# A transformer kernel on one core: three norm boundaries get a fixed order on three engines

## The chip, the core and the metric

The kernel runs on one core of a Trainium2 chip. Its engines are TensorE (PE, with its weight loads PEld), VectorE (DVE), ScalarE (ACT), GpSimd (POOL) and SyncE (SP, which issues the weight transfers). The metric is the device time of one launch in microseconds; the kernel before took 2123.85 us (median of three runs, 2120.73 to 2124.13).

## The reference

512 tokens of width 1024 pass through two models one behind the other, in float32. The first is one block of sparse attention and retention with an MLP. The second has two layers: an mLSTM mixer with a convolutional FFN, then a shared key and value projection, then a forgetting attention ("fox") with a second convolutional FFN. In the second model each sublayer is

```
y = mixer(rmsnorm(x, g_pre));  x = x + rmsnorm(y, g_post)
h = rmsnorm(x, g_ffn);         x = x + rmsnorm(conv_ffn(h), g_ffn_post)
```

with `rmsnorm(x, g) = x * rsqrt(mean(x*x) + 1e-6) * g`. So behind each mixer and each FFN a product's result is normed over its 1024 columns, added to x, and x is normed again for the next product.

## The kernel before

Activations lie with features on the 128 partitions: x is eight tiles of 128 x 512 (`xt[0..7]`), one column per token. Each float32 operand is split into a rounded part and a remainder (`hi`, `lo` for activations by `split`, `wh`, `wl` for weights by `split_steps`, L153 to L174), and a product is three matmuls, hi·wh, lo·wh and hi·wl (`mm3`, L474 to L476).

Weights come in blocks of up to 2048 columns a partition, in the order in which the products use them (`WT.plan`). SP loads a block into one of two `raw` buffers. A block is split in parts of 1024: ACT writes `wh`, DVE subtracts to get `wl`, or POOL does where `on_pool` lists the part: three parts at each of the three boundaries below. There are four buffers for `wh` and four for `wl`. `WT.get` loads and splits one block ahead.

`post_norm` ends a mixer or an FFN: a product with eight output tiles, whose last block (two tiles of 8 k steps behind a mixer, one tile of 22 k steps behind an FFN) is done in two halves of 256 tokens (`gemm_halves`). For each output tile ACT squares it (`sq`), DVE copies it from PSUM (`Y`), and POOL adds the squares up. When the first half of the last tile is done, `finish(0)` sums the squares over features (PE transposes, a DVE reduction), takes root (ACT) and reciprocal (DVE), and PE spreads the factor over a PSUM tile. Then, for each of eight rows k and each half: DVE scales Y (L1432), DVE adds it to x (L1434), ACT writes `hi` of the next product (L1438), DVE writes `lo` (L1439).

The next product is `gemm` with `lead=2`: its first two blocks, four output tiles, are multiplied in halves before the factor of its own norm is known. Each of the 16 k steps (8 a half) needs one row's `hi` and `lo`. Meanwhile `stats` squares x, sums it and computes 1 / sqrt with a shift and three Newton steps on DVE (`rsqrt`); the four results are copied aside and scaled later.

There are three such boundaries: behind the mLSTM mixer (into FFN 0), behind FFN 0 (into the key and value projection), and behind the fox mixer (into FFN 1). The last FFN ends in `last_norm`, which is another code.

The order of the instructions on an engine is chosen by the framework's scheduler with its own costs, by readiness and by the order in the program, except where `in_order` chains the instructions of given engines in program order; the second model's FFN regions chain POOL alone.

Of the kernel before, what the change touches and what calls it, by code (L numbers as in the profile page):

```python
# [14 lines left out]
OP = mybir.AluOpType  # L15
# [99 lines left out]
class Weights:  # L115
# [40 lines left out]
    def split_steps(self, i):  # L156
# [7 lines left out]
        for k0 in range(0, kt, kk):  # L164
# [8 lines left out]
                res.append(tuple(t[:, k * cols:(k + 1) * cols].bitcast(F32R) for t in (h, l)))  # L173
            yield  # L174

    def _split(self, i):
        if i not in self.parts and i < len(self.plan):
            for _ in self.split_steps(i):
                pass

    def get(self, ahead=True):
        i = self.pos
        self.pos += 1
        self._dma(i)
        self._split(i)
        self._dma(i + 1)
        if not ahead:
            return self.parts[i]
        self._split(i + 1)
        self._dma(i + 2)  # L190
        return self.parts[i]
# [3 lines left out]
def block_kernel(ctx: ExitStack, tc: tile.TileContext, I, out):  # L195
    nc = tc.nc
    V, A, G, T = nc.vector, nc.scalar, nc.gpsimd, nc.tensor

    cst = ctx.enter_context(tc.tile_pool(name="cst", bufs=1))
    up = ctx.enter_context(tc.tile_pool(name="up", bufs=1))  # L200
    sm = ctx.enter_context(tc.tile_pool(name="sm", bufs=12))
    wr = ctx.enter_context(tc.tile_pool(name="wr", bufs=2))
    wh = ctx.enter_context(tc.tile_pool(name="wh", bufs=4))
    pg = ctx.enter_context(tc.tile_pool(name="pg", bufs=4, space=bass.MemoryType.PSUM))
    pss = ctx.enter_context(tc.tile_pool(name="pss", bufs=2, space=bass.MemoryType.PSUM))
    pst = ctx.enter_context(tc.tile_pool(name="pst", bufs=1, space=bass.MemoryType.PSUM))
# [3 lines left out]
    def unit(name="u", tag=None, dt=F32):  # L210
        tag = tag or TAGS.get(name, "u")
        return up.tile([128, 512], dt, tag=tag, name=name, bufs=BUFS[tag])

    def R(t):
        return t.bitcast(F32R)
# [65 lines left out]

    def plan_ffn(l):
        W = I["ffn_w_up_2"][l]
        WT.on_pool((1, 0), (1, 1), (3, 0))
        for b in range(22):
            WT.add(8, 256, [(lambda v: v[:, :, 0:128], ksrc(W, 0, 8, b * 128, 128)),
                            (lambda v: v[:, :, 128:256], ksrc(W, 0, 8, 2816 + b * 128, 128))])
        WT.add_fm(I["ffn_w_down_2"][l], 22, 4, 0, tail=True)

    plan_ffn(0)  # L290
    WT.on_pool((0, 1), (1, 0), (1, 1))
    WT.add_fm(kvw, 8, 2, 0)
    WT.add_tok(kvw, 1792, 272)
    WT.add_fm(kvw, 8, 2, 512)
# [67 lines left out]
    def gcol(nm, k, layer=0):  # L362
        b = vbase[nm] + layer * 8 + k
        return gv[:, b:b + 1]
# [38 lines left out]
    def tick(ns):  # L403
        if side[0] is not None:
            side[0].tick(ns)
# [9 lines left out]
    def token_sums(tiles, h=None):  # L415


        n = len(tiles)
        u = small(4 if h is None else 2, "ts")
        for b in (0, 1) if h is None else (h,):  # L420
            p = s_bank()
            for i in range(2):
                for m, t in enumerate(tiles):
                    c = 256 * b + 128 * i
                    T.transpose(p[:, (i * n + m) * 128:(i * n + m + 1) * 128], t[:, c:c + 128], ident)
            o = u[:, 2 * b:2 * b + 2] if h is None else u
            V.tensor_reduce(o, p[:, 0:256 * n].rearrange("p (i c) -> p i c", i=2), axis=AX.X, op=OP.add)
        return u
# [26 lines left out]
    def rstd_col(acc):  # L455
        u = token_sums(acc)
        V.tensor_scalar(u, u, 1.0 / 1024.0, 1e-6, op0=OP.mult, op1=OP.add)
        return rsqrt(u)
# [38 lines left out]
    def gemm(acts, nb, evac, lead=0, mid=None, halves=False, rest=None):  # L497

        KT = len(acts)
        b = 0
        if lead:
            w = [WT.get() for _ in range(lead)]
            m = mid() if mid else None
            if m:
                next(m)
            ps = [g_bank() for _ in range(2 * lead)]  # L510
            for ts in thalf if halves else (slice(0, 512),):
                for k in range(KT):
                    for c in range(2 * lead):
                        mm3(ps[c][:, ts], cut(w[c // 2][k], c % 2), [t[:, ts] for t in acts[k]], k == 0, k == KT - 1)
                        if c % 2:
                            tick(1280)
            if m:
                rest = settle(ps, m, evac)
            else:
                for c in range(2 * lead):  # L520
                    evac(c, ps[c])
            b = lead
        while b < nb:
            if KT <= 8:
                w = WT.get()
                for c in range(2):
                    ps = g_bank()
                    with in_order(tc, (mybir.EngineType.PE,)) if rest else nullcontext():
                        for k in range(KT):
                            mm3(ps, cut(w[k], c), acts[k], k == 0, k == KT - 1)  # L530
                            if k % 2:
                                tick(1280)
                        if rest:
                            rest()
                            rest = None
                    evac(2 * b + c, ps)
            else:
                ps = [g_bank(), g_bank()]
                for k0 in range(0, KT, 8):
                    w = WT.get()  # L540
                    for k in range(len(w)):
                        for c in range(2):
                            mm3(ps[c], cut(w[k], c), acts[k0 + k], k0 + k == 0, k0 + k == KT - 1)
                        tick(1280)
                for c in range(2):
                    evac(2 * b + c, ps[c])
            b += 1
        return rest

    thalf = (slice(0, 256), slice(256, 512))  # L550

    def gemm_halves(acts, n0, evac):

# [828 lines left out]
    def post_norm(acts, nm, layer, pre):  # L1382


        Y, acc, last = [], [], []
        n0 = 6 if len(acts) == 8 else 7
        res = [(unit("hi"), unit("lo")) for _ in range(8)] if pre else None

        def f(n, ps):
            y = unit("Y")  # L1390
            sq = unit("sq", "u" if n == 0 else None)
            A.activation(sq, ps, AF.Square)  # L1392
            V.tensor_copy(y, ps)
            Y.append(y)
            if n == 0:
                acc.append(sq)
            else:
                G.tensor_tensor(acc[0], acc[0], sq, op=OP.add)  # L1398

        def f2(n, h, ps):  # L1400
            ts = thalf[h]
            if h == 0:
                Y.append(unit("Y"))
                last.append(unit("sq"))
            sq = last[n - n0]
            A.activation(sq[:, ts], ps, AF.Square)
            V.tensor_copy(Y[n][:, ts], ps)
            if n == 7:
                steps.append(finish(h))
                next(steps[h])  # L1410
                if h:
                    for g in steps:
                        for _ in g:
                            pass
            else:
                G.tensor_tensor(acc[0][:, ts], acc[0][:, ts], sq[:, ts], op=OP.add)

        steps = []

        def finish(h):  # L1420

            ts = thalf[h]
            sd = token_sums([acc[0], last[-1]], h)
            A.activation(sd, sd, AF.Sqrt, scale=1.0 / 1024.0, bias=eps)
            V.reciprocal(sd, sd)
            pb = (o_bank if h else t_bank)()
            for i in range(2):
                T.transpose(pb[:, i * 128:(i + 1) * 128], sd[:, i:i + 1].to_broadcast([128, 128]), ident)
            for k in range(8):
                if k == (0 if h else 4):  # L1430
                    yield
                V.scalar_tensor_tensor(Y[k][:, ts], Y[k][:, ts], gcol(nm, k, layer), pb[:, 0:256],  # L1432
                                       op0=OP.mult, op1=OP.mult)
                V.tensor_tensor(xt[k][:, ts], xt[k][:, ts], Y[k][:, ts], op=OP.add)  # L1434
                if pre is not None:
                    hi, lo = res[k]
                    g = gcol(pre[0], k, pre[1])
                    A.activation(R(hi[:, ts]), xt[k][:, ts], AF.Copy, scale=g)  # L1438
                    V.scalar_tensor_tensor(R(lo[:, ts]), xt[k][:, ts], g, hi[:, ts], op0=OP.mult, op1=OP.subtract)  # L1439

        if n0 == 6:
            gemm(acts, 3, f, lead=2)
            drain()
        else:
            wide_and_6(acts, f)
        gemm_halves(acts, n0, f2)
        return res

    def last_norm(acts, nm, layer):
# [61 lines left out]
    def stats(done):  # L1511
        acc = sumsq2(xt)
        yield
        rc = rstd_col(acc)
        done(rc, None)
        yield
        done(rc, bcast(rc))
# [204 lines left out]
```

## Time and profile before

| | |
|---|---|
| median of three runs | 2123.85 us |
| the profiled execution | 2121.7 us, span 2120.0 us, granted clock 0.996 |
| PE busy, share of the span | 2069.6 us, 98% |
| DVE, ACT, POOL busy | 1187.6, 947.7, 346.4 us |
| matmuls of the three products in `mm3` | 7812 of 10378, 2957 us of overlapping spans |
| weight loads by SP in blocks | 5.0 to 5.5 us from issue to landing |

Matmuls are pipelined, so their spans overlap and their number times their mean exceeds the time; the distance of their starts is what one costs. A share of 98% says that PE hardly idles, not that it runs at its peak.

### The profile page before, as it was taken

Reading aid. Unit: us, or ns where it says so; the run is one execution under the profiler, and the core shown is the slowest. Engines: PE = TensorE matmul, PEld = TensorE weight load, DVE = VectorE, ACT = ScalarE, POOL = GpSimd, SP = SyncE. Lnnn points to the kernel's source line nnn. Section 1 sums busy time; section 2 is a strip of 40 time slices with the busy share of each in tenths; the row PEclk is TensorE's granted clock in tenths of the full one; section 3 lists DMA queues with packets and bytes.
Section 4 is the critical chain, followed back from the end, with each engine's and each line's share of the span. In section 5 each row is a group of like instructions: output and inputs, shape, how many; then the busy total and the mean of one; then the engine's idle time right before and its main releaser. Section 6 shows DMA issues by size and latency. Waiting matters only on the chain.

```text
span 2120.0 us, 26605 instructions
## 1 busy us (share of the span) xinstructions
PE 2069.6 (98%) x10378; PEld 1711.1 (81%) x10378; DVE 1187.6 (56%) x2025; ACT 947.7 (45%) x1624; POOL 346.4 (16%) x369
## 2 busy tenths in 40 slices
PE   8899999999999999999999999999999999999998
PEld 6677678888888888887888888889877788888887
DVE  6955446545333335777597664256456468766422
ACT  5665533244323324555354443234467445444322
POOL 5431000002101201320221110021122022111000
PEclk9999999999999999999999999999999999999999
DMA  6331112432233332422423332233422232333222
GB/s 169 104 91 50 55 45 80 139 99 87 93 99 100 100 100 78 133 84 79 127 80 100 100 100 90 82 89 111 139 75 65 88 102 80 100 100 99 90 82 68
DMA packets 242030, 198.75 MB, mean 94 GB/s; under 512 B 15182, under 2 KB 232986, under 8 KB 241904
## 3 DMA queue, kind: packets, MB, share of 16 engines
q1 hardware_dynamic: 237808, 186.11, 29.3%
q0 software_dynamic: 4096, 10.94, 1.6%
q8 instruction: 81, 1.33, 0.3%
q14 instruction: 45, 0.37, 0.1%
HBM read 190.69 MB, written 6.34 MB: 93 GB/s over the span
## 4 chain that ended last, share of the span: by engine, by line
PE 50%; DVE 3%; ACT 1%; issue 1%; DMA 0%; POOL 0%; DVEq 0%; ACTq 0%; POOLq 0%
PE g L474 14%; PE g L475 14%; PE g L476 14%; PE o L1632 1%; PE t L874 1%; PE g L580 1%; PE g L581 1%; PE g L582 1%; DVE x L1434 1%; PE s L855 1%; PE s L856 0%; DVE Y L1432 0%; PE s L1455 0%; DVE wl L171 0%; DVE nt L435 0%
## 5 line engine op out<-in xcount | busy, mean ns | idle before, releaser
L474 PE MATMUL g<-hi,wh 128*128 128x512 f32 (+1 forms) x2604 | 993.1, 382 | 4.8 <-ACT wh L169 2.0
L476 PE MATMUL g<-hi,wl 128*128 128x512 f32 (+1 forms) x2604 | 982.3, 377 | 6.7 <-DVE wl L171 4.8
L475 PE MATMUL g<-lo,wh 128*128 128x512 f32 (+1 forms) x2604 | 981.8, 377 | 6.4 <-DVE lo L1439 6.4
L171 DVE TENSOR_TENSOR wl<-raw,wh 128x1024 fp32r<-128x1024 f32 (+3 forms) x339 | 411.5, 1216 | 380.9 <-ACT wh L169 378.1
L169 ACT ACTIVATE wh<-raw 128x1024 fp32r<-128x1024 f32 (+3 forms) x348 | 355.8, 1025 | 500.2 <-PE g L475 425.0
L474 PEld LDWEIGHTS g<-hi,wh 128*128 128x128 f32 x2604 | 491.7, 189 | 105.7 <-issue 15.5
L476 PEld LDWEIGHTS g<-hi,wl 128*128 128x128 f32 x2604 | 492.2, 189 | 96.9 <-DVE wl L171 7.3
L475 PEld LDWEIGHTS g<-lo,wh 128*128 128x128 f32 x2604 | 492.7, 189 | 92.2 <-DVE lo L1439 7.4
L863 ACT ACTIVATE P<-P,mx 128x128 f32<-128x128 f32 (+3 forms) x128 | 71.6, 560 | 35.9 <-DVE mx L861 34.9
L580 PE MATMUL g<-wh,hi 128*128 128x384 f32 (+3 forms) x256 | 85.7, 335 | 1.3 <-ACT mv L1241 1.2
L582 PE MATMUL g<-wl,hi 128*128 128x384 f32 (+3 forms) x256 | 83.5, 326 | 0.0
L581 PE MATMUL g<-wh,lo 128*128 128x384 f32 (+3 forms) x256 | 83.4, 326 | 0.0
L1150 POOL TENSOR_TENSOR relu<-relu 128x512 f32<-128x512 f32 x32 | 40.8, 1280 | 219.0 <-ACT relu L1149 213.9
L877 ACT COPY PT<-t 128x512 f32<-128x512 f32 (+1 forms) x96 | 48.6, 506 | 28.1 <-PE t L874 27.1
L1398 POOL TENSOR_TENSOR sq<-sq 128x512 f32<-128x512 f32 x16 | 27.0, 1685 | 203.5 <-ACT sq L1392 203.1
L372 DVE TENSOR_TENSOR lo<-relu,hi 128x512 fp32r<-128x512 f32 x32 | 22.1, 690 | 67.6 <-ACT hi L371 67.6
L861 DVE CUSTOM_DVE_ANT_0 P<-s,cdiag 128x128 f32<-128x128 f32 (+1 forms) x64 | 30.8, 489 | 50.6 <-PE s L856 46.8
L874 PE MATMUL t<-ident,P 128*128 128x128 f32 x320 | 52.7, 276 | 0.9 <-ACT PT L877 0.7
L580 PEld LDWEIGHTS g<-wh,hi 128*128 128x128 f32 x256 | 48.1, 188 | 5.8 <-issue 2.8
L452 POOL TENSOR_TENSOR sq<-sq 128x512 f32<-128x512 f32 x12 | 18.1, 1512 | 204.2 <-ACT sq L448 199.5
L861 DVE CUSTOM_DVE_ANT_0 P<-s,cb 128x128 f32<-128x128 f32 (+1 forms) x64 | 30.4, 488 | 36.0 <-PE s L858 26.6
L874 PEld LDWEIGHTS t<-ident,P 128*128 128x128 f32 x320 | 37.9, 140 | 14.1 <-ACT PT L877 6.9
(935 smaller groups left out, 2174.5 us busy)
## 6 DMA issues: line engine op xcount, KB each, us to landing
raw<-in_ffn_w_up_dram SPq DMA_DIRECT2D x88, 512.0 KB, 5.0
raw<-in_w_in_dram SPq DMA_DIRECT2D x16, 1024.0 KB, 5.2
raw<-in_w_up_dram SPq DMA_DIRECT2D x16, 1024.0 KB, 5.5
raw<-in_w_down_dram SPq DMA_DIRECT2D x16, 1024.0 KB, 5.0
raw<-in_ffn_w_down_dram SPq DMA_DIRECT2D x12, 1024.0 KB, 5.0
raw<-in_mlstm_w_in_dram SPq DMA_DIRECT2D x8, 1024.0 KB, 5.3
raw<-in_fox_w_qg_dram SPq DMA_DIRECT2D x8, 1024.0 KB, 5.3
raw<-in_ffn_w_down_dram SPq DMA_DIRECT2D x6, 768.0 KB, 4.3
```

Of the source, the lines that this page charges most:

```text
L169: self.nc.scalar.activation(h[:, 0:b - a].bitcast(F32R), raw[:, a:b], AF.Copy)
L171: e.tensor_tensor(l[:, 0:b - a].bitcast(F32R), raw[:, a:b], h[:, 0:b - a], op=OP.subtract)
L474: T.matmul(ps, lhsT=h, rhs=R(ah), start=first, stop=False)
L475: T.matmul(ps, lhsT=h, rhs=R(al), start=False, stop=False)
L476: T.matmul(ps, lhsT=l, rhs=R(ah), start=False, stop=last)
L580: T.matmul(ps[i][:, 0:cols], lhsT=R(ah)[:, ts], rhs=h, start=first, stop=False)
L581: T.matmul(ps[i][:, 0:cols], lhsT=R(al)[:, ts], rhs=h, start=False, stop=False)
L582: T.matmul(ps[i][:, 0:cols], lhsT=R(ah)[:, ts], rhs=l, start=False, stop=last)
L861: V.tensor_tensor_reduce(out=pr[:, 0:L], in0=ps[:, 0:L], in1=cdiag[:, 512 - L:512] if cb is None else cb[:, 0:L], scale=1.0, scalar=3e38, ...
L863: A.activation(pr[:, 0:L], pr[:, 0:L], AF.Exp, scale=-1.0, bias=mx, accum_out=rs[:, i, g:g + 1])
L874: T.transpose(pt[:, c + (i - j) * 128:c + (i - j + 1) * 128], P[i][:, j * 128:(j + 1) * 128], ident)
L877: A.copy(t[:, 0:c], pt[:, 0:c])
```

## The change

1. From the last block of `post_norm` to the end of the lead product behind it, the instructions of PE, DVE and ACT are chained in program order (`in_order`). `finish` is taken apart into jobs, set at counted k steps of the second half (`jobs`) and, as the generator `tail`, at the k steps of the lead product.
2. The two blocks of the lead product are loaded together (`next_two`) and split in four steps at given places. No part is split by POOL at these boundaries any more.
3. In `stats` the Newton steps are replaced by ACT's square root and DVE's reciprocal.
4. The SBUF pools are allocated in another order, with a filler of 384 bytes, so that the large tiles start at multiples of 2 KB.

The diff, cut to its core (the removed `finish` is the old text of the same steps):

```diff
+    def next_two(self):
+        for i in (self.pos, self.pos + 1):
+            self._dma(i)
+        return [self.split_steps(i) for i in (self.pos, self.pos + 1)]
...
+        if ahead is None:
+            return self.parts[i]
...
-        WT.on_pool((1, 0), (1, 1), (3, 0))
-    WT.on_pool((0, 1), (1, 0), (1, 1))
...   (gemm, lead)
+            tail = behind.pop() if behind else None
+            w = [WT.get(None if tail else True) for _ in range(lead)]
...
                 for k in range(KT):
+                    if tail:
+                        next(tail, None)
                     for c in range(2 * lead):
                         mm3(...)
+            if tail:
+                next(tail, None)
+                for i in (WT.pos, WT.pos + 1):
+                    WT._dma(i)
+                WT._split(WT.pos)
+                next(m)
...   (post_norm)
+        def root(h):
+            sd[h] = token_sums([acc[0], last[-1]], h)
+            A.activation(sd[h], sd[h], AF.Sqrt, scale=1.0 / 1024.0, bias=eps)
+        def factor(h):
+            pb[h] = (o_bank if h else t_bank)()
+            for i in range(2):
+                T.transpose(pb[h][:, i * 128:(i + 1) * 128], sd[h][:, i:i + 1].to_broadcast([128, 128]), ident)
+        def root0():
+            root(0)
+            V.reciprocal(sd[0], sd[0])
+        def part(n):
+            return lambda: next(e[n])
+        def row(h, k):
+            V.scalar_tensor_tensor(Y[k][:, ts], Y[k][:, ts], gcol(nm, k, layer), pb[h][:, 0:256], ...)
+            V.tensor_tensor(xt[k][:, ts], xt[k][:, ts], Y[k][:, ts], op=OP.add)
+            A.activation(R(hi[:, ts]), xt[k][:, ts], AF.Copy, scale=g)
+            V.scalar_tensor_tensor(R(lo[:, ts]), xt[k][:, ts], g, hi[:, ts], op0=OP.mult, op1=OP.subtract)
...
+        order = in_order(tc, (mybir.EngineType.PE, mybir.EngineType.DVE, mybir.EngineType.Activation))
+        order.__enter__()
+        e = WT.next_two()
+        next(e[0])
+        if n0 == 6:
+            next(e[1])
+        if n0 == 6:
+            jobs = {4: [root0], 10: [factor0, row0(0), row0(1)], 13: [row0(2)]}
+            left = [row0(3), part(0), part(1), row0(4)]
+        else:
+            jobs = {4: [root0], 10: [factor0, row0(0), part(1)], 13: [row0(1), row0(2)], 17: [part(0), row0(3)]}
+            left = [part(1), row0(4)]
+        for h, ts in enumerate(thalf):
+            for n, w in enumerate(ws, n0):
+                ps = g_bank()
+                for k in range(KT):
+                    if h:
+                        for job in jobs.get(count, ()):
+                            job()
+                        count += 1
+                    mm3(ps[:, 0:256], w[k], [t[:, ts] for t in acts[k]], k == 0, k == KT - 1)
+                f2(n, h, ps[:, 0:256])
+        def tail():
+            for job in left:
+                job()
+            for g in e:
+                next(g, None)
+            yield
+            root(1)
+            yield
+            row(0, 5)
+            yield
+            V.reciprocal(sd[1], sd[1])
+            row(0, 6)
+            yield from wait(3)
+            factor(1)
+            row(0, 7)
+            for k in range(8):
+                row(1, k)
+            yield from wait(10)
+            order.__exit__(None, None, None)
+            yield
...   (stats)
-        rc = rstd_col(acc)
+        rc = token_sums(acc)
+        A.activation(rc, rc, AF.Sqrt, scale=1.0 / 1024.0, bias=eps)
+        V.reciprocal(rc, rc)
```

## Rows read from the trace of the kernel before

**Rows 1.** The page: busy time of each engine, share of the span, instructions.

```profile
PE 2069.6 (98%) x10378; PEld 1711.1 (81%) x10378; DVE 1187.6 (56%) x2025; ACT 947.7 (45%) x1624; POOL 346.4 (16%) x369
```

**Rows 2.** Waits of PE, whole run: us in total, times, longest.

```profile
PE g L475 <- DVE lo L1439: 6.4, 4, 2.0
...
PE s L425 <- ACT sq L1406: 2.6, 1, 2.6
PE t L463 <- DVE ny L440: 2.4, 2, 1.2
...
PE g L476 <- POOL wl L171: 1.9, 1, 1.9
```

**Rows 3.** Stages A, B, C: length, busy time by engine, clock, DMA share, GB/s.

```profile
1039.84:1074.57 34.73, 30.97 (x254) 30.22 (x253) 30.70 (x61) 19.27 (x36) 8.32 (x5) 1.00 0.18 47
1407.58:1447.08 39.50, 34.95 (x273) 34.34 (x272) 31.02 (x60) 19.25 (x36) 10.65 (x5) 0.91 0.18 52
1725.29:1761.59 36.30, 33.52 (x255) 32.60 (x254) 30.77 (x61) 19.28 (x36) 8.30 (x5) 0.91 0.18 48
```

**Rows 4.** Timeline of PE, stage B: start, length, instruction (22 starts, first and last).

```profile
1444.44 0.28 PE L476 MATMUL g<-hi,wl 128*128 128x256 f32 x1
...
1446.96 0.28 PE L476 MATMUL g<-hi,wl 128*128 128x256 f32 x1
```

**Rows 5.** Busy time in short stretches, columns as in rows 3.

```profile
88.00:92.00 4.00, 1.45 (x5) 0.86 (x5) 3.97 (x5) 3.73 (x5) 1.57 (x1) 1.00 0.00 0
...
1424.00:1426.00 2.00, 2.00 (x11) 2.00 (x11) 2.00 (x7) 0.75 (x3) 0.00 (x0) 0.50 0.63 224
```

**Rows 6.** Timeline of POOL, stage A.

```profile
1046.31 4.88 POOL L171 TENSOR_TENSOR wl<-raw,wh 128x1024 fp32r<-128x1024 f32 x2 [1.48 <-DVE Y L1432]
```

**Rows 7.** Timeline of DVE, stages A and C.

```profile
1046.66 2.31 DVE L1439 SCALAR_TENSOR_TENSOR lo<-x,gv,hi 128x256 fp32r<-128x256 f32 x1
...
1053.25 0.68 DVE L427 TENSOR_REDUCE ts<-s 128x2 f32<-128x512 f32 x1
...
1054.24 0.41 DVE L1434 TENSOR_TENSOR x<-x,Y 128x256 f32<-128x256 f32 x1
1054.58 0.15 DVE L1425 RECIPROCAL ts<-ts 128x2 f32<-128x2 f32 x1
...
1056.49 0.47 DVE L1432 SCALAR_TENSOR_TENSOR Y<-Y,gv,t 128x256 f32<-128x256 f32 x1
1056.88 0.47 DVE L1439 SCALAR_TENSOR_TENSOR lo<-x,gv,hi 128x256 fp32r<-128x256 f32 x1
...
1756.67 0.48 DVE L1439 SCALAR_TENSOR_TENSOR lo<-x,gv,hi 128x256 fp32r<-128x256 f32 x1 [1.03 <-ACT hi L1438]
```

**Rows 8.** Timeline of DVE near the start: an operation and its user.

```profile
24.43 0.69 DVE L630 SCALAR_TENSOR_TENSOR ang<-nturn,ang 128x512 f32<-128x512 f32 x1
25.16 0.69 DVE L631 SCALAR_TENSOR_TENSOR ang<-nturn,ang 128x512 f32<-128x512 f32 x1
```

**Rows 9.** Timeline of ACT, stages A and C.

```profile
1053.96 0.30 ACT L1424 ACTIVATE ts<-ts,eps 128x2 f32<-128x2 f32 x1 [1.54 <-DVE ts L427]
1054.69 0.51 ACT L1438 ACTIVATE hi<-x,gv 128x256 fp32r<-128x256 f32 x1 [0.43 <-DVE x L1434]
...
1756.14 0.49 ACT L1438 ACTIVATE hi<-x,gv 128x256 fp32r<-128x256 f32 x1
1756.55 1.05 ACT L169 ACTIVATE wh<-raw 128x1024 fp32r<-128x1024 f32 x1
```

**Rows 10.** Timeline of PE, stage A: the factor's two transposes.

```profile
1043.67 0.38 PE L1428 MATMUL t<-ident,ts 128*128 128x128 f32 x2
```

**Rows 11.** Instructions of line 171 near stage A: shortest, median, longest ns.

```profile
L171 DVE TENSOR_TENSOR wl<-raw,wh x7: 1210/1217/1226, 1032.4 to 1094.9; 128x1024 fp32r<-128x1024 f32 x7
```

**Rows 12.** Timeline of PE, products of 272 columns (34 starts, first and last).

```profile
845.78 0.29 PE L582 MATMUL g<-wl,hi 128*128 128x272 f32 x1
...
849.95 0.28 PE L582 MATMUL g<-wl,hi 128*128 128x272 f32 x1
```

More of the change, by code (lines that the diff above doesn't have):

```diff
@@ L197, in block_kernel @@
     V, A, G, T = nc.vector, nc.scalar, nc.gpsimd, nc.tensor
-    cst = ctx.enter_context(tc.tile_pool(name="cst", bufs=1))
-    up = ctx.enter_context(tc.tile_pool(name="up", bufs=1))
     sm = ctx.enter_context(tc.tile_pool(name="sm", bufs=12))
+    gap = ctx.enter_context(tc.tile_pool(name="gap", bufs=1))
+    gap.tile([128, 96], F32, name="gap")
     wr = ctx.enter_context(tc.tile_pool(name="wr", bufs=2))
     wh = ctx.enter_context(tc.tile_pool(name="wh", bufs=4))
+    up = ctx.enter_context(tc.tile_pool(name="up", bufs=1))
+    cst = ctx.enter_context(tc.tile_pool(name="cst", bufs=1))
     pg = ctx.enter_context(tc.tile_pool(name="pg", bufs=4, space=bass.MemoryType.PSUM))
@@ L505, in gemm @@
         if lead:
-            w = [WT.get() for _ in range(lead)]
+            tail = behind.pop() if behind else None
+            w = [WT.get(None if tail else True) for _ in range(lead)]
             m = mid() if mid else None
-            if m:
+            if m and not tail:
                 next(m)
@@ L550, in block_kernel @@
     thalf = (slice(0, 256), slice(256, 512))
+    behind = []
     def gemm_halves(acts, n0, evac):
@@ L1385, in post_norm @@
         Y, acc, last = [], [], []
-        n0 = 6 if len(acts) == 8 else 7
-        res = [(unit("hi"), unit("lo")) for _ in range(8)] if pre else None
+        KT = len(acts)
+        n0 = 6 if KT == 8 else 7
+        res = [(unit("hi"), unit("lo")) for _ in range(8)]
         def f(n, ps):
@@ L1407, in f2 @@
             V.tensor_copy(Y[n][:, ts], ps)
[L1408 to L1415, printed above, removed]
-                G.tensor_tensor(acc[0][:, ts], acc[0][:, ts], sq[:, ts], op=OP.add)
-        steps = []
-        def finish(h):
-            ts = thalf[h]
[L1423 to L1439, printed above, removed]
@@ new lines, in f2 @@
+            if n < 7:
+                G.tensor_tensor(acc[0][:, ts], acc[0][:, ts], sq[:, ts], op=OP.add)
+        sd, pb = [None, None], [None, None]
+        def root(h):
[5 more added lines that the diff above has]
+                T.transpose(pb[h][:, i * 128:(i + 1) * 128], sd[h][:, i:i + 1].to_broadcast([128, 128]), ident)
@@ new lines, in root0, with factor0, row0 @@
+        def root0():
+            root(0)
+            V.reciprocal(sd[0], sd[0])
+        def factor0():
+            factor(0)
+        def row0(k):
+            return lambda: row(0, k)
+        def part(n):
+            return lambda: next(e[n])
+        def row(h, k):
+            ts = thalf[h]
+            V.scalar_tensor_tensor(Y[k][:, ts], Y[k][:, ts], gcol(nm, k, layer), pb[h][:, 0:256],
+                                   op0=OP.mult, op1=OP.mult)
+            V.tensor_tensor(xt[k][:, ts], xt[k][:, ts], Y[k][:, ts], op=OP.add)
+            hi, lo = res[k]
+            g = gcol(pre[0], k, pre[1])
+            A.activation(R(hi[:, ts]), xt[k][:, ts], AF.Copy, scale=g)
+            V.scalar_tensor_tensor(R(lo[:, ts]), xt[k][:, ts], g, hi[:, ts], op0=OP.mult, op1=OP.subtract)
@@ L1445, in post_norm @@
             wide_and_6(acts, f)
-        gemm_halves(acts, n0, f2)
+        order = in_order(tc, (mybir.EngineType.PE, mybir.EngineType.DVE, mybir.EngineType.Activation))
+        if n0 == 6:
+            w = WT.get(False)
+            ws = [[cut(v, c) for v in w] for c in range(2)]
+        else:
+            ws = [sum((WT.get(k0 + 8 < KT) for k0 in range(0, KT, 8)), [])]
+        order.__enter__()
[3 more added lines that the diff above has]
+            next(e[1])
+        if n0 == 6:
+            jobs = {4: [root0], 10: [factor0, row0(0), row0(1)], 13: [row0(2)]}
+            left = [row0(3), part(0), part(1), row0(4)]
+        else:
+            jobs = {4: [root0], 10: [factor0, row0(0), part(1)], 13: [row0(1), row0(2)], 17: [part(0), row0(3)]}
+            left = [part(1), row0(4)]
+        count = 0
+        for h, ts in enumerate(thalf):
[28 more added lines that the diff above has]
+            yield
+        behind.append(tail())
         return res
```

## The prediction

> **What bounds the kernel now.** I read the page's busy line first: PE 2069.6 of 2120.0 us [rows 1], so only what stops PE, or slows it, counts. The wait table of PE over the whole run comes next: of the waits that belong to the three norms in the change, 6.4 us end on `lo`, 2.6 on a late `sq`, 2.4 on the Newton steps and 1.9 on a weight split by POOL [rows 2]. Third, the busy time by stage, from the last matmul of the first half of the last column block to the end of the first product behind the norm. I call these stages A (mLSTM mix), B (first FFN) and C (fox mix): 34.73, 39.50 and 36.30 us [rows 3].
>
> What PE alone needs there comes from its matmul spacing: 21 steps of 256 columns take 2.52 us, 0.12 each [rows 4]. A and C hold 48 matmuls of the second half, 192 of the lead product and 12 transposes: 252 x 0.12 = 30.24 us. B has 66 in its second half: 270 x 0.12 = 32.40. So PE loses 4.49, 7.10 and 6.06 us, part of it at the lower clock in B and C (granted 0.91 over the stage, 0.50 in the worst stretch, against 1.00 in A) [rows 3, 5].
>
> The stall's source: while POOL splits two weights (4.88 us), a `lo` on DVE takes 2.31 us instead of 0.47 [rows 6, 7]. DVE is busy for 30.7 us of 34.73 in A [rows 3]: it is the second bound there, and the change must be judged by what DVE and ACT do per row.
>
> **A row in the fixed order.** The change chains PE, DVE and ACT in the order in which the code issues them, from the start of the last block to the end of the lead product. `row(h, k)` issues Y, x (DVE), hi (ACT), lo (DVE). Y feeds x, x feeds hi, hi feeds lo, and the next row's Y stands behind lo on DVE. Before, the planner set other rows' work between them, and a row cost DVE only its issue spacing: Y to lo 0.39, x to its successor 0.34, lo like Y (each some 0.08 less than its length [rows 7]), so 0.39 + 0.34 + 0.39 = 1.12 us.
>
> In the fixed order each wait shows. Dependent neighbours on DVE: an operation of 0.69 starts at 24.43, its user at 25.16, which is 0.04 after the end [rows 8]. x ends at 1054.65 and hi starts at 1054.69; a hi ends at 1756.63 (1756.14 + 0.49) and the lo that waits for it starts at 1756.67 [rows 7, 9]. A row is then Y 0.47 + 0.04, x 0.41 + 0.04, hi 0.49 + 0.04, and 0.39 until the next Y: 1.88 us. PE uses up a row of the lead product in 12 x 0.12 = 1.44 us. DVE becomes the bound, and what stands behind each waiting lo is everything DVE has left.
>
> The Trainium skill ("VectorE: DVE Perf Modes", § The DRAIN you can't avoid) says that each operation waits until the pipe is empty, and that a semaphore costs nothing more. By that a dependent pair would cost no more than another, and the 48 rows would be 48 x 0.12 = 5.8 us cheaper. The rows differ: an independent neighbour starts 0.08 before the end, a dependent one 0.04 after it [rows 7, 8]. The measurement decides.
>
> **Sum for A and C**, from the end of the first half. Before `factor0` PE issues ten k steps (30 matmuls) and root's 4 transposes, 34 x 0.12 = 4.08 us. Factor's transposes end 0.38 after their start [rows 10]; with 0.06 for the handover Y of row 0 starts at 4.52. On DVE follow 16 rows, 30.08; the copy of the last block, 0.34 (like x); the two parts split in `left`; root(1)'s reduction, 0.68 less the overlap, 0.60; the reciprocal, 0.08 [rows 7]. The parts: behind hi of row 3 ACT makes `wh`, which ends 0.97 after that hi (it starts 0.08 before hi's end and takes 1.05 [rows 9]); 0.04 later DVE starts the first `wl`, 1.22 long [rows 11] and, less the overlap of 0.08, 1.14 ahead of the second, which follows at once. Of 0.97 + 0.04 + 2 x 1.14 DVE would have used the first 0.43 for lo anyway: 2.86. Sum 4.52 + 30.08 + 0.34 + 2.86 + 0.60 + 0.08 = 38.48. The last k step follows, 1.44 and 0.03 of handover: 39.95 us, against 34.73 (+5.22) and 36.30 (+3.65).
>
> **Sum for B.** There are 22 k steps, and three parts are split between rows: two cost 0.97 + 0.04 + 1.14 - 0.43 = 1.72 each; the third has the last `sq` before its `wh` on ACT (0.30 more) and takes the copy into its wait, 2.0 with the copy. 4.52 + 30.08 + 3.44 + 2.0 + 0.60 + 0.08 + 1.47 = 42.19 us against 39.50: +2.69. In B PE would stop longest at one place: root(1)'s transposes stand before the second k step, and their `sq` stands on ACT behind hi of row 3, some 15 us into the stage, when PE is there at about 10. That idle time is inside the sum, since DVE ends later still.
>
> **The other edits.** Square root and reciprocal replace 13 small DVE instructions. In A and C PE no longer waits for the Newton steps, 1.2 us each: -2.4 [rows 2]. The new pair is an ACT operation of 0.30 and a DVE one of 0.15 [rows 7, 9], far shorter than 13 dependent ones at 0.15 + 0.04 or more. No POOL splits: 9 splits go to DVE at 1.14; two in A and C and three in B are in the sums, and the fourth chunk's falls behind the stage, where DVE has time. The DMAs of the two next blocks are issued at the stage's start and those of the next pair behind the lead product; SP carries only weights there, and the chain does not bind it. A buffer comes free after the last split, some 15 us into the stage, and has 24 us until it is needed: 0. If the scheduler put them late, a stage would lose at most the split's 2.3.
>
> Squares, their sums on DVE (four a stage) and the next block's two splits lie outside the chain. In DVE's holes of a row they cost nothing, ahead of a row or of the token sums up to two `wl`, 2.3 a stage: 0 to 6.9. I take 0, since in each row DVE stands idle for 0.57 us, and keep 6.9 for the range.
>
> Tiles at 2 KB: products of 272 columns read rows 1088 bytes apart, so at changing offsets, and step at 4.17 / 33 = 0.1264 us; 272 / 2.4 GHz is 113.3 ns, so 13.1 ns are over, and for 256 columns 120 - 106.7 = 13.3 [rows 4, 12]. With a spread of 0.2 ns over 10378 matmuls alignment is worth 2 us at most in either direction: 0.
>
> Total: 5.22 + 2.69 + 3.65 - 2.4 = +9.2 us. The profiled execution took 2121.7 us (1.7 around its span), so 2130.9; it lies 2.15 under the median of 2123.85, on which the same sum gives 2133.0. I predict 2133.
>
> **Rivals.**
> Faster: PE never waits. This is right if a row costs DVE under 1.44 us, PE's rate; that point decides. For it speaks that the interleaved row took 1.12 and that POOL's blocking goes. Against it stands that lo needs hi, and hi needs x, in every row, with nothing between. Price: 4.49 + 7.10 + 6.06 + 2.4 = 20.0 us less: 2103.8 by the median.
>
> No change: the row costs some 1.69 us (shorter handovers, or rows prepared during the second half count for more); 48 x 0.19 = 9.1 takes the loss back: 2124.
>
> Much slower: PE's clock. At the lower level a k step takes 2.88 us, more than DVE's 1.88. If each lead product ran so throughout, PE would set the pace again: 16 x 1.00 us more a stage, 48 in all: 2181. The Trainium skill ("TensorE: Matmul & The Clock Gate", § HAM oscillation — how this bites in real kernels) has a kernel whose clock falls at each repeated wait. The trace has PE busy for 1.45 of 4 us near 90 us with 1.00 granted [rows 5], and gaps of 0.44 a step are far smaller. One low stretch in h = 0 costs little, as DVE sets the end.
>
> **How the numbers follow.** Forecast 0.66, with its own range 2127 (x behind Y at the spacing of independent neighbours, 0.39 for 0.51, in 48 rows) to 2140 (6.9 for squares and splits); much slower 0.04; no change 0.15; faster 0.15. A difference under 0.2%, 4.2 us, can't be told from none. Part of the forecast's low edge falls within that, so faster 0.16, same 0.17, slower 0.67. The range 2112 to 2143 leaves out most of the faster case and the clock case, about 2 in 10.
>
> **What would show it.** Right: in the lead products the chain alternates DVE x, ACT hi, DVE lo; a row's Y starts come 1.8 to 1.95 us apart; PE waits for `lo` in most k steps (0.4 us each) and once for `sq` at root(1), longest in B; `lo` and x never take 2 us; no wait for `ny` in A and C. Wrong: rows closer than 1.5 us, or a stage under 33 us. The sum is wrong in size if other DVE work stands between rows, or if PEclk is 0.5 through a stage.

## The result, and the profile after

The changed kernel takes 2147.26 us (median of four runs, 2146.91 to 2147.84), the kernel before 2123.99 beside it: 1.0117 of before, interval 1.0103 to 1.0131, or 23.3 us more. The sign is as forecast; the size is 2.5 times the 9.2 us of the sum, and 4.3 us above the range. The profiled execution took 2147.49 us, 25.8 more than the one before.

The page of the changed kernel, engines' busy time [rows 1]:

```profile
PE 2085.5 (97%) x10378; PEld 1719.9 (80%) x10378; DVE 1184.9 (55%) x1998; ACT 949.4 (44%) x1627; POOL 324.6 (15%) x360
```

The three stages of the changed kernel, cut as in [rows 3], with the same columns:

```profile
1039.96:1086.18 46.22, 37.55 (x257) 34.07 (x255) 32.25 (x63) 19.88 (x36) 4.32 (x3) 0.93 0.23 69
1417.59:1465.40 47.81, 38.16 (x275) 35.72 (x274) 31.97 (x63) 19.76 (x36) 2.58 (x2) 0.93 0.16 46
1743.16:1789.39 46.23, 37.65 (x256) 34.10 (x255) 32.27 (x63) 19.87 (x36) 4.32 (x3) 0.93 0.24 69
```

A, B and C grew by 11.49, 8.31 and 9.93 us, 29.7 together; forecast were 5.22, 2.69 and 3.65. The rest of the program became 3.9 us shorter (ahead of A it is 0.1 longer; the stretches behind the stages went from 333.01 to 331.41, 278.21 to 277.76 and 358.41 to 356.41 us), and 29.7 - 3.9 is the 25.8 of the two spans. So the three stages hold all of the loss, and the question is what stands in them. PE's waits over the whole run, to be set beside [rows 2]:

```profile
PE g L483 <- DVE Y L1427: 12.0, 3, 6.2
PE g L483 <- ACT hi L1462: 9.8, 12, 1.9
...
PE g L484 <- DVE lo L1463: 2.1, 3, 0.9
```

The waits for `ny`, for a late `sq` and for GpSimd's `wl` are gone, and in the lead products PE now waits more for `hi` than for `lo`. New is a wait for `Y` of L1427, once a stage: the copy that empties the PSUM bank of the last tile, which the fourth tile of the lead product needs.

What DVE does is seen in its timeline in stage A: first row 0 of the first half up to the next row's Y, then rows 3 to 5 of the second half (start, length, operation, in brackets the idle time before it and what ended that). Row (h, k) is row k of half h, counted from 0:

```profile
1044.41 0.48 DVE L1457 SCALAR_TENSOR_TENSOR Y<-Y,gv,t 128x256 f32<-128x256 f32 x1
1044.93 0.42 DVE L1459 TENSOR_TENSOR x<-x,Y 128x256 f32<-128x256 f32 x1
1045.93 0.48 DVE L1463 SCALAR_TENSOR_TENSOR lo<-x,gv,hi 128x256 fp32r<-128x256 f32 x1 [0.58 <-ACT hi L1462]
1046.33 0.48 DVE L1457 SCALAR_TENSOR_TENSOR Y<-Y,gv,t 128x256 f32<-128x256 f32 x1
...
1069.28 0.47 DVE L1457 SCALAR_TENSOR_TENSOR Y<-Y,gv,o 128x256 f32<-128x256 f32 x1
1069.79 1.23 DVE L1459 TENSOR_TENSOR x<-x,Y 128x256 f32<-128x256 f32 x1
1071.59 0.48 DVE L1463 SCALAR_TENSOR_TENSOR lo<-x,gv,hi 128x256 fp32r<-128x256 f32 x1 [0.58 <-ACT hi L1462]
1071.99 0.47 DVE L1457 SCALAR_TENSOR_TENSOR Y<-Y,gv,o 128x256 f32<-128x256 f32 x1
1072.39 0.68 DVE L461 TENSOR_TENSOR sq<-sq 128x512 f32<-128x512 f32 x1
1072.99 0.42 DVE L1459 TENSOR_TENSOR x<-x,Y 128x256 f32<-128x256 f32 x1
1074.05 1.22 DVE L171 TENSOR_TENSOR wl<-raw,wh 128x1024 fp32r<-128x1024 f32 x1 [0.65 <-ACT wh L169]
1075.20 0.48 DVE L1463 SCALAR_TENSOR_TENSOR lo<-x,gv,hi 128x256 fp32r<-128x256 f32 x1
1075.59 0.47 DVE L1457 SCALAR_TENSOR_TENSOR Y<-Y,gv,o 128x256 f32<-128x256 f32 x1
1075.98 1.22 DVE L171 TENSOR_TENSOR wl<-raw,wh 128x1024 fp32r<-128x1024 f32 x1
1077.12 1.49 DVE L1459 TENSOR_TENSOR x<-x,Y 128x256 f32<-128x256 f32 x1
1079.18 0.48 DVE L1463 SCALAR_TENSOR_TENSOR lo<-x,gv,hi 128x256 fp32r<-128x256 f32 x1 [0.58 <-ACT hi L1462]
1079.58 0.48 DVE L1457 SCALAR_TENSOR_TENSOR Y<-Y,gv,o 128x256 f32<-128x256 f32 x1
```

An undisturbed row takes 1.92 us from Y to Y, of which DVE stands idle for 0.58 before lo. Row (1,3) takes 2.71, (1,4) 3.60, (1,5) 3.99, and (1,6) and (1,7) 0.48 more than an undisturbed one each. What lengthens them is not part of the rows: the sums of squares of the next norm (L461) and the next block's two `wl` (L171). They are issued behind the chain in the code, the chain does not hold them, and the scheduler set them into it. It set three of DVE's four adds between Y and x (the fourth stands behind the last row). There they push back x, so hi, so lo, and the 0.58 before lo stays idle all the same. The long x of 1.23 and 1.49 us have another cause, seen in GpSimd's timeline of the same stretch:

```profile
1069.44 1.29 POOL L461 TENSOR_TENSOR sq<-sq 128x512 f32<-128x512 f32 x1 [24.77 <-ACT sq L457]
1076.03 2.30 POOL L461 TENSOR_TENSOR sq<-sq 128x512 f32<-128x512 f32 x1 [5.29 <-ACT sq L457]
```

While GpSimd adds (until 1070.73 and 1078.33), x on DVE does not finish. The second add is itself held up: a `wl` on DVE starts just ahead of it, at 1075.98, and it takes 2.30 us in place of 1.29. Stage B shows which operations are hit:

```profile
1456.52 1.29 POOL L461 TENSOR_TENSOR sq<-sq 128x512 f32<-128x512 f32 x1 [4.67 <-ACT sq L457]
```

```profile
1456.53 0.48 DVE L1457 SCALAR_TENSOR_TENSOR Y<-Y,gv,o 128x256 f32<-128x256 f32 x1
1457.04 1.05 DVE L1459 TENSOR_TENSOR x<-x,Y 128x256 f32<-128x256 f32 x1
```

The Trainium skill ("SBUF — State Buffer", § SBUF: two separate sides) has a lock for this: a DVE operation with two inputs from SBUF and a GpSimd operation that reads SBUF shut each other out for a whole instruction. Here the trace agrees: x, with two inputs in SBUF, ends about 0.3 us behind the adds, while Y, which reads its factor from PSUM, keeps its 0.48 us beside an add that starts 0.01 us ahead of it.

### The profile page after: what moved, and what is told of

It is laid out like the page before. It is cut to its first block, busy times and chain, and to the rows that moved or that the text cites. A ratio compares the mean times of both kernels' runs of the same rounds, so it can differ in the third digit from the quotient of the medians.

```text
span 2145.8 us, 26563 instructions
## 1 busy us (share of the span) xinstructions
PE 2085.5 (97%) x10378; PEld 1719.9 (80%) x10378; DVE 1184.9 (55%) x1998; ACT 949.4 (44%) x1627; POOL 324.6 (15%) x360
## 5 line engine op out<-in xcount | busy, mean ns | idle before, releaser
L171 DVE TENSOR_TENSOR wl<-raw,wh 128x1024 fp32r<-128x1024 f32 (+3 forms) x348 | 422.5, 1216 | 384.3 <-ACT wh L169 381.4
L461 POOL TENSOR_TENSOR sq<-sq 128x512 f32<-128x512 f32 x12 | 19.1, 1594 | 267.6 <-ACT sq L457 267.3
L1462 ACT ACTIVATE hi<-x,gv 128x256 fp32r<-128x256 f32 x48 | 24.4, 508 | 68.1 <-DVE x L1459 65.2
```

The source lines that it names most:

```text
L171: e.tensor_tensor(l[:, 0:b - a].bitcast(F32R), raw[:, a:b], h[:, 0:b - a], op=OP.subtract)
```

## The experiments

**The small edits, one at a time, on the kernel before.** First square root and reciprocal:

```diff
-        rc = rstd_col(acc)
+        rc = token_sums(acc)
+        A.activation(rc, rc, AF.Sqrt, scale=1.0 / 1024.0, bias=eps)
+        V.reciprocal(rc, rc)
```

> The kernel before with one part of the change alone: square root and reciprocal in place of the Newton steps behind the three lead products. Theory: PE's wait for the last Newton step, 1.2 us each behind stages A and C, goes and nothing takes its place: 2.4 us less, 2121.6. Second reading, from the stretches behind the three stages in the two traces (333.01 to 331.41, 278.21 to 277.76, 358.41 to 356.41 us): all of these 4.05 us belong to this edit, 2120.0. Rival: the wait was cover for something else that is late anyway (the weights of the next block), 2124.

Measured: 2120.49 against 2121.07 us, ratio 0.9995 (0.9986 to 1.0003). The wait for `ny` is gone and the stretches behind the stages took 331.64, 278.18 and 357.08 us, 2.7 less than before, so the step works as described. The times show less of it and can't tell it from nothing. In this profile stage A took 36.30 us at a granted clock of 0.91, where [rows 3] have 34.73 at 1.00; the profiled execution of before, with its clock at the upper level throughout A, lay 2.3 us under its median.

Second, no splits by GpSimd:

```diff
-        WT.on_pool((1, 0), (1, 1), (3, 0))
-    WT.on_pool((0, 1), (1, 0), (1, 1))
```

> The kernel before with one part alone: GpSimd splits no weights at the three boundaries, DVE does all nine parts. Theory: DVE takes 2.3 us more of splits in A and C and 3.4 in B, but lo and x no longer wait for GpSimd (2.31 us in place of 0.47); with the scheduler free to interleave, the two come out near even: 2122 (2119 to 2126). Rival: DVE is the second bound (30.7 busy of 34.73 us), so its added 2.3, 3.4 and 2.3 us all lengthen the stages: 2131 to 2132.

Measured: 2130.86 us, 1.0047 (1.0035 to 1.0060), the rival's time. A took 36.93 us and C 36.91, both at a granted clock of 1.00. Where the splits stay on GpSimd, the stages at 1.00 are A with 34.73 [rows 3] and C with 34.67 (in `align_alone`, below): 2.2 us less, and the rival had 2.3. B is not as the rival has it. It took 46.03 us, 6.5 more than in [rows 3] where 3.4 were expected, and PE's waits there show one piece:

```profile
PE g L474 <- DVE wl L171: 11.3, 1, 11.3
```

It ends at 1433.64 us, 25 us into the stage: with nothing to hold it, the scheduler put a `wl` of the lead product itself behind nearly all rows on DVE.

Third, the pools in the other order (the fourth part of the change, alone):

```diff
-    cst = ctx.enter_context(tc.tile_pool(name="cst", bufs=1))
...
+    gap = ctx.enter_context(tc.tile_pool(name="gap", bufs=1))
+    gap.tile([128, 96], F32, name="gap")
```

> The kernel before with one part alone: the SBUF pools in the other order with the filler, so that the large tiles start at 2 KB. Theory: nothing, 2124 within 1 us. Rival: matmuls and vector operations read faster or slower by 0.2 ns or more each, 2122 or 2126.

Measured: 2121.47 us, 1.0001 (0.9992 to 1.0010). No difference from the kernel before, as said.

**The fixed order itself.** The changed kernel, DVE and ACT taken out of the chain:

```diff
-        order = in_order(tc, (mybir.EngineType.PE, mybir.EngineType.DVE, mybir.EngineType.Activation))
+        order = in_order(tc, (mybir.EngineType.PE,))
```

> The changed kernel with the chain on PE alone; DVE and ACT are left to the scheduler, all other edits stay. Theory: the fixed order on DVE and ACT is what costs. The scheduler sets another row's Y or x between x and lo, a row costs DVE some 1.2 to 1.3 us in place of 1.91, the stages fall from 46.2, 47.8 and 46.2 to 35 to 38 us, in all some 30 us less: 2117 (2110 to 2124). Rival: the other edits (no splits by GpSimd, PE's own fixed order with root(1) and the late bank) or the lower clock in the stages cost the time: 2140 or more.

Measured: 2107.70 us, 0.9942 (0.9929 to 0.9956). The stages of this kernel:

```profile
1038.42:1072.38 33.96, 32.44 (x255) 31.83 (x253) 28.45 (x63) 19.16 (x36) 4.12 (x3) 0.95 0.22 64
1404.39:1438.48 34.09, 32.49 (x272) 32.28 (x271) 28.69 (x63) 19.27 (x36) 3.40 (x2) 1.00 0.17 45
1716.52:1748.93 32.41, 30.89 (x255) 30.28 (x253) 28.45 (x63) 19.16 (x36) 4.13 (x3) 1.00 0.23 68
```

and DVE in its stage A, in the second half, where other rows' work now fills the wait for hi:

```profile
1060.79 0.42 DVE L1459 TENSOR_TENSOR x<-x,Y 128x256 f32<-128x256 f32 x1
1061.12 0.86 DVE L1457 SCALAR_TENSOR_TENSOR Y<-Y,gv,o 128x256 f32<-128x256 f32 x2
1061.90 0.47 DVE L1463 SCALAR_TENSOR_TENSOR lo<-x,gv,hi 128x256 fp32r<-128x256 f32 x1
1062.30 0.75 DVE L1459 TENSOR_TENSOR x<-x,Y 128x256 f32<-128x256 f32 x2
```

The chain on DVE and ACT costs the difference: 39.6 us by the medians, 36.6 if each is set against the kernel before that ran beside it, and 39.8 in the stages (140.3 against 100.5), so all of it lies there. What DVE's chain costs alone, and what ACT's, was not tried. Without both the other edits beat the kernel before.

**Where the added work stands.** The chain reaches on over the next split and the squares:

```diff
-                next(tail, None)
...
                 WT._split(WT.pos)
                 next(m)
+                next(tail, None)
```

> The changed kernel with the chain reaching further: the next block's split and the squares with their sums are chained too, and so stand behind the last row on DVE and ACT. Theory: these are what stretches rows (1,3) to (1,7) from 1.91 to 2.39 to 3.99 us; the rows go back to 1.91 and the stages to 40.7, 43.9 and 40.7 us (14.9 us less). Of it PE gives back some 1.5 us a stage, since the next block's wl now comes about 2.3 us after the last hi and the lead product has 1.4 us left then: 2137 (2133 to 2142). Rival: the rows are slow for another reason in the second half (clock, PE's reads), and stay over 2.4 us: 2147 or more.

Measured: 2155.41 us, 1.0159 (1.0145 to 1.0174), 18 us above the expectation; yet the stages were 40.45, 43.76 and 40.49 us, where 40.7, 43.9 and 40.7 were expected. The loss lies behind them: the three stretches took 338.87, 284.66 and 364.90 us, 7.5, 6.9 and 8.5 more than in the changed kernel. On PE, behind the lead product:

```profile
1087.00 1.84 PE L434 MATMUL s<-ident,sq 128*128 128x128 f32 x7 [5.62 <-DVE sq L461]
```

The transposes of the token sums stand ahead of the next block in PE's queue and wait for the sums that were pushed back; this wait is 5.6 of A's 7.5 us, and the changed kernel has none there. So it is shown what lengthens the rows, and I had missed a user of the sums.

The same work at other places, written out between x and lo, all sums on DVE (the diff is cut to the place in the row; the squares are issued row by row and the next loads earlier too):

```diff
             A.activation(R(hi[:, ts]), xt[k][:, ts], AF.Copy, scale=g)
+            if hole:
+                hole()          # an add in rows (1,3), (1,4), (1,7); a wl in rows (1,5), (1,6)
             V.scalar_tensor_tensor(R(lo[:, ts]), xt[k][:, ts], g, hi[:, ts], op0=OP.mult, op1=OP.subtract)
```

> The changed kernel with the same work in other places: the sums of squares (all on DVE, none on GpSimd) and the next block's two wl are written out between x and lo of a row, where DVE waits 0.58 us for hi, or behind the last row. Theory: the place is what costs, not the work. Between Y and x an add delays hi and with it lo by 0.48; between x and lo it is nearly free (0.60 against 0.58), a wl costs 0.6 and x is not blocked by GpSimd. Stages A and C 42 us, B 44.5: some 12 us less, 2135 (2132 to 2139). Rival: DVE has to find the 4.7 us a stage wherever they stand: 2145 to 2149.

Measured: 2134.01 us, 1.0060 (1.0046 to 1.0073); stages 41.37, 42.69 and 41.43. DVE, rows (1,3) and (1,5):

```profile
1068.74 0.43 DVE L1488 TENSOR_TENSOR x<-x,Y 128x256 f32<-128x256 f32 x1
1069.09 0.68 DVE L1482 TENSOR_TENSOR sq<-sq 128x512 f32<-128x512 f32 x1
1069.75 0.48 DVE L1494 SCALAR_TENSOR_TENSOR lo<-x,gv,hi 128x256 fp32r<-128x256 f32 x1
...
1072.92 1.22 DVE L192 TENSOR_TENSOR wl<-raw,wh 128x1024 fp32r<-128x1024 f32 x1
1074.06 0.48 DVE L1494 SCALAR_TENSOR_TENSOR lo<-x,gv,hi 128x256 fp32r<-128x256 f32 x1
```

lo starts 1.01 behind x with the add between them, 1.00 without: an add in the idle time costs nothing. With all added work set there, or behind the last row, the kernel is 12.5 us over the kernel before beside it, where the sum had 9.2 and the changed kernel has 23.3. Two things changed at once, the place of the work and the engine of two adds. By the rows of the changed kernel GpSimd's two adds blocked x for 1.7 of the 4.9 us that A gained, so by this estimate the place is worth some 3.

How much of it are the sums, how much the splits? This kernel leaves the additions out and makes only the squares:

```diff
-        acc = sumsq2(xt)
+        acc = sumsq2(xt, adds=False)
```

> The changed kernel without the sums of squares behind the three norms: the eight squares are made, but not added up (only the last two enter the factor); the next block's splits stay where they were. It splits what the rows lose into two halves. Theory: in stage A the sums cost 3.2 us (row (1,3) 0.80 for an x blocked by GpSimd, rows (1,4), (1,6) and (1,7) 0.48 each for an add between Y and x, row (1,5) 0.94 for another blocked x), the two wl the other 2.3; in B 2.9, in C 3.2. Stages A and C 43.0, B 44.9, in all 9.3 us less: 2138 (2136 to 2140). Rival: the wl alone hold up the rows and the adds ride in their shadow: less than 4 us gained, 2143 or more.

Measured: 2139.22 us, 1.0078 (1.0064 to 1.0092); stages 43.13, 44.95 and 44.74. A and B are as worked out. In A 3.1 us go with the sums, some 0.3 of them at its end, where the changed kernel's clock was low; the two rows that hold the two `wl` stay 2.7 us longer than undisturbed ones. C is 1.7 longer than worked out: its last k steps ran at a lower clock (granted 0.76 from the last lo to the end, 3.01 us; in A 1.00 and 1.48).

**A row that does not wait.** lo of row k issued behind x of row k+1, still in the chain:

```diff
-            V.scalar_tensor_tensor(R(lo[:, ts]), xt[k][:, ts], g, hi[:, ts], ...)
+            flush()             # the lo of the row before
+            late.append(lambda: V.scalar_tensor_tensor(R(lo[:, ts]), xt[k][:, ts], g, hi[:, ts], ...))
```

> The changed kernel with one shift in the fixed order: lo of row k is issued behind x of row k+1, so that hi is made meanwhile and DVE does not stand for it. Squares, sums and splits are left where the scheduler puts them. Theory: the wait for hi, 0.58 us in each of 16 rows, is what makes DVE the bound: a row costs 0.51 + 0.34 + 0.39 = 1.24 us in place of 1.91, 10 us less a stage, which come to 36 to 38 us: 2117 (2111 to 2123). Rival: PE's wait for the bank of the last tile (2.9, 6.2, 2.9 us) or its lower clock sets the stage, and little is won: 2135 or more.

Measured: 2127.14 us, 1.0024 (1.0014 to 1.0033), 4 us above the expected range; stages 37.66, 42.86 and 37.74. Rows come 1.25 us apart, A and C are as expected, B is not:

```profile
1436.01 0.48 DVE L1463 SCALAR_TENSOR_TENSOR Y<-Y,gv,o 128x256 f32<-128x256 f32 x1 [3.71 <-PE o L1440]
```

In B PE waits 4.5 us for the last tile's bank. The transposes of the second factor stand behind that in PE's fixed order, and so DVE waits for them in turn. In the changed kernel the same loop cost 1.3 us in B (a wait of 1.23 for `o`). I moved the copy forward:

```diff
-            jobs = {4: [root0], 10: [factor0, row0(0), part(1)], 13: [row0(1), row0(2)], 17: [part(0), row0(3)]}
-            left = [part(1), row0(4)]
+            jobs = {4: [root0], 10: [factor0, row0(0), part(1)], 13: [row0(1), row0(2)]}
+            left = [part(0), row0(3), part(1), row0(4)]
```

> The kernel pipe with one more shift, at the boundary behind FFN 0 alone: a weight part and row 3 of the first half move behind the last tile's copy in the fixed order. Theory: in pipe's stage B the copy that frees the last tile's PSUM bank stands behind row 3 on DVE, PE waits 4.5 us for it, comes late to the transposes of the second factor, and DVE then waits 3.7 us for those. With the copy some 4 us earlier both waits shrink to about 1 us, stage B goes from 42.9 to 39 us, the other stages stay: 2123 (2121.5 to 2125). Rival: the second factor's place in PE's order is what binds, or the split moved behind the copy costs as much again: 2126 to 2129.

Measured: 2124.58 us, 1.0013 (1.0004 to 1.0023). The time is as the theory has it, but B went to 41.22, not 39, less than half of the way. PE's wait for the bank fell from 4.5 to 0.9 us and DVE's for the second factor from 3.7 to 2.1, but PE now waits 4.1 us for `lo`, where it waited 1.8 in `pipe`. The bank is part of it; that the moved row and split cost the rest is likely by these waits, and no run shows it.

**What the other edits are worth without the chain.** No chain on PE either:

```diff
-        order.__enter__()
...
-            order.__exit__(None, None, None)
```

> The changed kernel without any chain: PE too is left to the scheduler, the other edits stay. Theory: PE's fixed order matters little, since PE only waits 1.4 to 1.6 us a stage in pe_chain; within 4 us of pe_chain, 2104 to 2112. Rival: PE's chain is what keeps the transposes of the two roots and factors in good places; without it PE runs into them too early, as in the kernel before, and the gain of pe_chain over the kernel before is lost: 2120 or more.

Measured: 2106.41 us, 0.9924 (0.9911 to 0.9937); stages 32.35, 32.89 and 32.35. That is as the theory had it: PE's chain is worth nothing that these runs can tell.

GpSimd's splits back into pe_chain:

```diff
+        WT.on_pool((1, 0), (1, 1), (3, 0))
+    WT.on_pool((0, 1), (1, 0), (1, 1))
```

> The kernel pe_chain with GpSimd splitting weights at the three boundaries as in the kernel before. Theory: in pe_chain DVE has time (28.5 us busy of 32.4 to 34), so the splits by GpSimd only bring back the blocked lo and x (2.31 us in place of 0.47): 1 to 2 us a stage more, 2111 to 2114. Rival: what nopool_alone showed holds here too, DVE needs the relief, and it is faster by up to 9 us: 2099 to 2105.

Measured: 2122.11 us, 1.0001 (0.9992 to 1.0010): the whole gain is lost, 14.4 us, more than twice what I had allowed. In its stage B, GpSimd first, then DVE, then PE's wait:

```profile
1417.97 4.84 POOL L171 TENSOR_TENSOR wl<-raw,wh 128x1024 fp32r<-128x1024 f32 x2 [2.25 <-ACT wh L169]
```

```profile
1418.57 2.05 DVE L1465 SCALAR_TENSOR_TENSOR lo<-x,gv,hi 128x256 fp32r<-128x256 f32 x1
1420.54 2.89 DVE L1461 TENSOR_TENSOR x<-x,Y 128x256 f32<-128x256 f32 x2
...
1424.53 0.41 DVE L1429 COPY Y<-g 128x256 f32<-128x256 f32 x1
```

```profile
PE g L485 <- DVE Y L1429: 6.5, 1, 6.5
```

The blocked operations push back everything behind them on DVE, the bank's copy among it. In A and C PE's wait for that copy is 3.5 us each. The three make 13.5 us, against 4.4 in pe_chain, so 9.1 of the 12.9 us by which the stages grew lie in this one wait.

The bank's wait covered in pe_chain, by taking the fourth tile up three k steps late:

```diff
+                    first = tail and ts is thalf[0]
+                    for c, kk in ([(c, k) for c in range(3 if first and k < 3 else 4)] if not (first and k == 3)
+                                  else [(3, 0), (3, 1), (3, 2)] + [(c, 3) for c in range(4)]):
```

> The kernel pe_chain with the fourth output tile of the lead product three k steps late: its first three steps come ahead of the fourth of all. Theory: the wait for the bank of the last tile, 1.4 to 1.6 us in each of the three stages, is covered by the other three tiles, since the rows of the first k steps are ready; 4.4 us less, 2103.3, and up to 1.6 us more if stage A keeps its clock. Rival: lo of rows 1 to 3 is late then, and PE waits for these in place of the bank: 2107 to 2109.

Measured: 2105.80 us, 0.9923 (0.9910 to 0.9936); stages 32.00, 33.01 and 32.02, and no wait for the bank in PE's list. Of the 4.4 us of waits the medians show 1.9 as gain and the stages 3.4, part of that from A's clock (1.00 for 0.95). Waits for lo, 1.1 us in all, took some of it back, as the rival said. With `free` it is the fastest version here, 0.8% under the kernel before.

## Why the prediction was right in sign and wrong in size

**Right: the row and the sum along DVE.** I put 1.88 us on a row in the fixed order; it is 1.92. Each term of the sum for A, read off the starts of Y in the trace after: first Y at 4.45 us (forecast 4.52), copy 0.34 (0.34), the two parts 2.82 (2.86), the reduction 0.60 (0.60), the reciprocal 0.08 (0.08). In B the three parts cost 1.70, 1.69 and, with the copy, 1.96 (1.72, 1.72, 2.0). "DVE becomes the bound" holds: without the chain the stages come down to 32 to 34 us, where PE alone needs 30.24 to 32.40, and pe_chain is 13.4 us under the kernel before beside it, of the 20.0 that the faster rival gave for rows that don't hold PE.

**Wrong: "Squares, their sums on DVE (four a stage) and the next block's two splits lie outside the chain ... I take 0, since in each row DVE stands idle for 0.57 us".** This term measured 5.5 us in A and in C and 3.9 in B, 14.9 us of the 18.2 by which the stages passed my sum; even the 2.3 a stage kept for the range was too little. Three things were left out. I counted idle time, and not which side of it the added work falls on: an add between Y and x costs 0.48 of its 0.60, since hi then comes later by as much, and between x and lo it costs nothing (`holes`). A `wl`, 1.22 long, does not fit into that idle time: in the changed kernel the one between x and lo also waits for its `wh` and costs 1.2, the one between Y and x about 1; in `holes`, between x and lo with `wh` ready, one costs 0.5. And GpSimd's two sums block x for 0.8 and some 0.9 us in A, the same contention that I read in [rows 6, 7] for the splits and did not carry over to the sums that stay on GpSimd. `no_sums` shows both parts: about half of A's 5.5 us are the sums, the other half the two `wl`. The prediction had named the sign of this, "if other DVE work stands between rows", and still gave the term nothing.

**The rest of the 18.2 us.** The row, 0.035 us over in 48 rows: 1.7. The second factor in B, 1.3: I had said that PE's longest stop in B "is inside the sum, since DVE ends later still", but the second factor stands behind that stop and DVE needs it. I also named the wrong wait there: the stop of 6.2 us ends 15.9 us into the stage, about where I said, but on the bank's copy on DVE, not on `sq` at root(1). The end of A and C, about 0.3 each, where the lead product's last matmuls ran partly at the lower clock. The terms that came out smaller than forecast take back some 0.4 in all.

**The other edits.** Newton steps: -2.4 forecast; the stretches show -2.7, the runs -0.6 with an interval that reaches from nothing to both. The other 1.2 of the 3.9 us outside the stages I did not trace to an edit. Tiles at 2 KB: nothing, right. Leaving out GpSimd's splits gains 14.4 us where DVE and ACT are not chained (`pool_back` against pe_chain) and costs 9.8 in the kernel before, most of it in B with its one late `wl`: one edit, both signs, by what else fixes the order.

**The clock.** PE idled more, yet the granted clock was 0.93 in each stage (a mean over its two levels, 1.2 and 2.4 GHz), against 1.00, 0.91 and 0.91 before, and the row on DVE kept its time: the rival of 2181 was rightly small. Its price was too high besides, since I only doubled the k step, to 2.88 us. At the lower level, in stage B of the kernel before, 14 steps of 256 columns lie between these two starts:

```profile
1424.01 0.41 PE L474 MATMUL g<-hi,wh 128*128 128x256 f32 x1
...
1427.00 0.41 PE L476 MATMUL g<-hi,wl 128*128 128x256 f32 x1
```

That is 0.2136 us each, so 2.56 for a k step and some 2166 for the rival.

The Trainium skill ("TensorE: Matmul & The Clock Gate", § HAM oscillation — how this bites in real kernels) has a kernel whose clock falls at each repeated wait. The trace agrees in part: the clock is 0.66 from 1050 to 1055 us, behind the 2.9 us stop for the bank, 1.00 from 1055 to 1080 us through waits of up to 1.9 us for hi and lo, and 0.50 from 1081 to 1084.4 us behind them. Nor is a short wait always without a fall: in C of `no_sums` the clock went to the lower level at 1771.4 us, behind waits of at most 0.9.

## What to carry to other kernels

A fixed order on an engine can turn each dependency in it into idle time there: write the row so that independent work stands between an operation and its user (lo of a row behind x of the next: 1.25 us in place of 1.92), or leave the engine to the scheduler. Work that the chain does not name is still put into it, so price it at the worst place and not by the idle time that exists, and ask of each wait who else stands behind it in the same queue. An edit's worth in one order (no splits by GpSimd, +9.8 us) says little of its worth in another (-14.4).

## What was not expected of the hardware

The same stage of the same code took 34.73 us at a granted clock of 1.00 in one profiled execution and 36.30 at 0.91 in another (stage A of the kernel before, and of it with the square root). In `align_alone` it is A that has 36.29 at 0.91 and C that has 34.67 at 1.00, the other way round than in [rows 3]. That is 1.6 us between executions that otherwise agree, as much as several of the edits are worth, so a stage read from one profile is no surer than that.
